# Modulation products of blocks 2 to 4 on the vector engine, an output product accumulated over two row blocks, and expert 0 with 64 slots: a diffusion layer with experts on one core

## The chip, the core and the metric

The kernel runs on one core of a Trainium2 chip. The metric is the device time of one execution in microseconds (us), the median of several runs. Everything is float32 in memory. The names of the engines are those of the profile: PE is the tensor engine (PEld its weight loads), DVE the vector engine, ACT the scalar engine, POOL the GpSimd, SP the queue that issues the weight loads.

## What is computed

One layer over 256 tokens of 2048 channels. A conditioning vector gives six modulation vectors of 2048 (mod[0] to mod[5]); a gated short convolution and a mixture of 16 experts (top group, then top two of its four experts) follow, each with a residual and a layer norm.

```python
mod = split(silu(c) @ mod_w + mod_b, 6)          # mod_w: 2048 x 12288
h = x * (1 + mod[1]) + mod[0]
gate_b, gate_c, val = split(h @ conv_in_w, 3)    # 2048 x 6144
o = (gate_b * depthwise_conv3(gate_c * val, conv_w)) @ conv_out_w
x = layer_norm(ALPHA * x + mod[2] * o, g0, b0)
h = x * (1 + mod[4]) + mod[3]                    # routed by h @ rt_grp_w, h @ rt_exp_w
y = sum over experts e of weight[e] * ((silu(h @ gate[e]) * (h @ up[e])) @ down[e])
x = layer_norm(ALPHA * x + mod[5] * y, g1, b1)   # gate, up: 2048 x 768, down: 768 x 2048
```

Evaluated on its inputs, the reference sends 14 tokens to expert 0 and 117, 80, 78, 51 and 42 to the five most loaded of the others.

## The kernel before

All weights pass once through one stream of loads on SP, in the order in which the work uses them. A ring of 6 tiles of 1.5 MB holds them (`RING`, line 30); two more places are lent to the stream late. `get` (line 118) issues the next load when the tile that had its place has been used. So a transfer starts when an engine lets go of an older tile.

**The convolution part.** float32 is split into a rounded half (cast by ACT, line 379) and the remainder (a subtraction on DVE, line 380), and three fast products replace a slow one (`mm3`, lines 387 to 389). The first product runs over eight groups of 256 channels (times three for gate_b, gate_c, val). For groups 0 to 3 it goes in five stages over the contraction (`KGS`, line 35: 2, 2, 4, 4 and 4 blocks of 128 rows), since mod[0] and mod[1] are made block by block on the way (`acc_step`, line 442; sums in four large tiles, copied there in the first stage, added later). At the end of each stage `h_hook` (line 557) empties DVE's queue (`flush`, line 544) and makes the next blocks of the modulated input (`make_h`, line 360: ACT gives the rounded half, DVE the product again and the remainder). Groups 4 to 7 run whole, in four steps each (`full_steps`, line 453). The output product `cout_step` (line 506) takes one of four row blocks (`qt`) and one of four column blocks (`j`) at a time; each of these 16 results is multiplied by mod[2] on DVE (line 531) and added to the tokens: on DVE for row blocks 0 and 3, on POOL for 1 and 2 (lines 533 to 537).

**The modulation vectors.** mod[0] and mod[1] are products on PE with 32 identical columns (`gemv_cols`, line 226, matmul at line 258). mod[2] is made by `gemv_rows` (line 275, matmul at 285) in four pieces of 512 columns. Of the eight pieces of mod[3] and mod[4], `ON_V` (line 40) puts five on DVE: the first block of 128 rows is a multiplication on ACT, the other 15 are `scalar_tensor_tensor` of 512 columns (line 263) that wait in `queue`; `split` (line 376) runs two of them (`VN`) after each weight split. A piece takes three loads (6, 6 and 4 blocks of 128 rows). mod[5] follows later, on PE.

**The order** is written out (lines 587 to 609). `EXTRA` says how many loads of mod[2] to mod[4] are put between the steps of each of the five stages, `merge` spreads them evenly, and `BEFORE` (line 36) says how many steps are left behind `router_prep`. Here 13 loads lie in the stages, 12 of them in the last, and 23 among the steps of groups 4 to 7 and eight output steps.

**The experts.** Rank 0 is expert 0, the others are ranked by load; `CAPS` (line 43) gives the slots of each rank: four with 128, four with 64, eight with 32. `SEQ` is the order: 0, 15, 14, 1, 13, 12, 2, 11, 10, 3, 9, 4, 7, 5, 6, 8. Tokens are gathered by a product with a one-hot matrix (`gather`, line 793). An expert has 8 loads for gate and up and 4 for down, 1.5 MB each. With 128 slots (`run_expert`, line 875) half of the gate and up blocks are split into two parts and done in three fast products, the other half as float32, and the down product is split by 256 columns (lines 949 to 954) with four pairs of buffers (line 685). With 64 or 32 slots all is float32, and two or four products stand side by side in the columns of PE (lines 904 and 947). `Alone` (line 970) takes the output of an expert with 128 slots back to the tokens, `Packed` (line 995) that of two or four smaller ones together. A loop (line 1175) runs once for each block of slots that a rank lacks.

Of the kernel before, what the change touches and what calls it, by code (L numbers as in the profile page):

```python
# [9 lines left out]
F32 = mybir.dt.float32  # L10
# [4 lines left out]
ALU = mybir.AluOpType  # L15
# [18 lines left out]
EXTRA = [0, 1, 0, 0, 12]  # L34
# [16 lines left out]
# Pieces of the columns of the down product; those of the last experts end with smaller ones.  # L51
# [14 lines left out]
def trunk_kernel(  # L66
# [36 lines left out]
    # ---------------------------------------------------------------- weight stream  # L103
# [14 lines left out]
    def get(i):  # L118
        """the tile of load i, whose predecessors have been used; issues what now has a place"""
# [24 lines left out]
    def expert_loads(e, pieces=QUARTERS):  # L144
        """loads of an expert's gate and up weights, and of its down weights by pieces of the columns"""
# [19 lines left out]
    # ---------------------------------------------------------------- constants, small inputs  # L165
# [10 lines left out]
    # picks rows 0, 32, 64 and 96  # L176
# [38 lines left out]
    # arithmetic that waits for its turn on the tensor engine, and on the vector engine  # L215
# [10 lines left out]
    def gemv_cols(m, c0, n, on_vector=False):  # L226
# [3 lines left out]
        nb, k0 = n // P, c0 // P  # L230

        def late():
            pt = aux_tile(f"gc{m}_{c0}")
            for i in range(nb):
                TE.transpose(pt[:, i * P : (i + 1) * P], box["r"][:, i * P : (i + 1) * P], ident)
            sm = const.tile([P, 4], F32, tag="gsum", bufs=2, name=f"gs{m}_{c0}")
            V.tensor_reduce(out=sm[:, :nb], in_=pt[:, :n].rearrange("p (i c) -> p i c", i=nb)[:, :, :: 1 if on_vector else 32],
                            axis=AX.X, op=ALU.add)
            V.scalar_tensor_tensor(
                out=modT[:, m, k0 : k0 + nb], in0=sm[:, :nb], scalar=1.0 if m in (1, 4) else 0.0,  # L240
                in1=modbT[:, m * KT + k0 : m * KT + k0 + nb], op0=ALU.add, op1=ALU.add)

        per = min(KT, 3072 // n)
        for t0 in range(0, KT, per):
            nt = min(per, KT - t0)

            def work(w, t0=t0, nt=nt):
                if t0 == 0:
                    if on_vector:
                        box["r"] = p1.tile([P, 512], F32, tag="rows", bufs=2, name=f"rows{m}{c0}")  # L250
                    else:
                        box["ps"] = aux_tile(f"gv{m}_{c0}")
                for k in range(nt):
                    kt = t0 + k
                    g = kt % 4
                    ws = w[:, k * n : (k + 1) * n]
                    if not on_vector:
                        TE.matmul(box["ps"][32 * g : 32 * g + 32, :n], sT[:, kt : kt + 1].to_broadcast([P, 32]), ws, start=kt < 4, stop=kt >= 12)  # L258
                    elif kt == 0:
                        S.mul(box["r"][:, :n], ws, sT[:, kt : kt + 1])  # L260
                    else:
                        def fn(ws=ws, kt=kt):
                            V.scalar_tensor_tensor(out=box["r"][:, :n], in0=ws, scalar=sT[:, kt : kt + 1],  # L263
                                                   in1=box["r"][:, :n], op0=ALU.mult, op1=ALU.add)
                            if kt == KT - 1:
                                pending.append(late)
                        queue.append(fn)
                if t0 + nt == KT and not on_vector:
                    box["r"] = p1.tile([P, 512], F32, tag="rows", bufs=2, name=f"rows{m}{c0}")
                    S.copy(box["r"][:, :n], box["ps"][:, :n])  # L270
                    pending.append(late)
# [963 lines left out]
```

## Time and profile before

| what | us |
|---|---|
| median of 3 runs (1347.04 to 1348.72) | 1348.4 |
| span of the profiled execution, first to last instruction | 1343.3 |
| PE busy | 1190.9 |
| DVE busy | 724.2 |
| ACT busy | 404.6 |

The runs are timed from outside the span; the profiled execution itself has no other time than its span, 5.1 us less than the median. Matmuls are pipelined, so a busy PE may also be waiting a little; how fast it goes is read from the starts of its matmuls. A window of the profile gives the busy time of every engine, the clock granted to PE (1.00 is 2.4 GHz), the share of the DMA engines and the rate in GB/s, for a stretch of time.

### The profile page before, as it was taken

How to read it: one execution, taken by the hardware profiler on the slowest of the kernel's cores; microseconds unless marked ns; L12 is line 12 of the kernel's file. 1: busy time of each engine (PE TensorE's matmuls, PEld its weight loads, DVE VectorE, ACT ScalarE, POOL GpSimd, SP SyncE). 2: the span in 40 equal slices, each digit the busy share in tenths (PEclk: the TensorE clock that was granted, in tenths of full speed). 3: DMA queues.
4: the chain of work that ended last, by engine and by line, in shares of the span. 5: the costliest groups of instructions: out<-in, count | busy, mean ns of one | idle time of the engine just before them, and what ended most of it. 6: DMA issues, size and time to landing. Idle time of an engine off the chain costs nothing. (4 is left out here: it accounts for less than half of the span.)

```text
span 1343.3 us, 23490 instructions
## 1 busy us (share of the span) xinstructions
PE 1190.9 (89%) x9429; PEld 856.0 (64%) x9429; DVE 724.2 (54%) x1526; ACT 404.6 (30%) x795; POOL 30.3 (2%) x60
## 2 busy tenths in 40 slices
PE   4999999999999999998789878997689888898883
PEld 2778876978699875775367446774267454554553
DVE  2665565597789878686266434583147321122217
ACT  1333333434244334563035223451026110100020
POOL 0000000000400120000000000000000000000000
PEclk7999999999999999999889899998789899999996
DMA  9999879799989879979999899989999999999992
GB/s 321 354 396 395 298 279 398 276 310 351 357 312 337 296 280 342 364 263 365 413 414 347 316 414 411 400 304 381 412 412 393 336 412 412 413 371 414 412 410 78
DMA packets 240947, 475.85 MB, mean 354 GB/s; under 512 B 10968, under 2 KB 74680, under 8 KB 240576
## 3 DMA queue, kind: packets, MB, share of 16 engines
q1 hardware_dynamic: 235808, 471.88, 93.2%
q10 hardware_dynamic: 5024, 2.40, 0.6%
q8 instruction: 76, 1.25, 0.3%
q14 instruction: 39, 0.32, 0.1%
HBM read 472.16 MB, written 2.10 MB: 353 GB/s over the span
## 5 line engine op out<-in xcount | busy, mean ns | idle before, releaser
L904 PE MATMUL gue<-w,xgp 128*32 128x384 f32 (+1 forms) x1536 | 218.1, 554 | 71.2 <-DMA w<-in_ex_w_up_dram 59.0
L387 PE MATMUL ci<-hhi,hic 128*128 128x256 f32 x768 | 221.1, 289 | 2.7 <-ACT hic L379 1.4
L389 PE MATMUL ci<-hhi,loc 128*128 128x256 f32 x768 | 218.6, 286 | 3.6 <-DVE loc L380 3.5
L388 PE MATMUL ci<-hlo,hic 128*128 128x256 f32 x768 | 217.9, 284 | 0.8 <-DVE hlo L374 0.7
L904 PEld LDWEIGHTS gue<-w,xgp 128*32 128x32 f32 (+1 forms) x1536 | 83.1, 130 | 197.8 <-issue 83.0
L693 DVE TENSOR_TENSOR parts<-w,parts 128x256 fp32r<-128x256 f32 (+1 forms) x320 | 135.3, 475 | 73.2 <-ACT parts L692 70.4
L692 ACT CAST parts<-w 128x256 fp32r<-128x256 f32 (+1 forms) x320 | 131.3, 449 | 114.5 <-PE gue L901 72.7
L379 ACT CAST hic<-w 128x1024 fp32r<-128x1024 f32 (+1 forms) x108 | 102.5, 954 | 183.2 <-PE ci L388 159.0
L387 PEld LDWEIGHTS ci<-hhi,hic 128*128 128x128 f32 x768 | 145.1, 189 | 14.9 <-issue 8.4
L389 PEld LDWEIGHTS ci<-hhi,loc 128*128 128x128 f32 x768 | 145.2, 190 | 9.5 <-DVE loc L380 6.0
L388 PEld LDWEIGHTS ci<-hlo,hic 128*128 128x128 f32 x768 | 146.4, 191 | 5.6 <-DVE hlo L374 2.5
L380 DVE TENSOR_TENSOR loc<-w,hic 128x1024 fp32r<-128x1024 f32 (+1 forms) x108 | 118.7, 1108 | 35.2 <-ACT hic L379 35.0
L921 ACT COPY gse<-gue 128x384 f32<-128x384 f32 x16 | 7.7, 480 | 314.8 <-PE gue L904 314.8
L904 PE MATMUL gue<-w,xfp 128*128 128x384 f32 x256 | 93.9, 498 | 2.5 <-DMA w<-in_ex_w_gate_dram 2.5
L1014 DVE TENSOR_TENSOR Y<-dne,m 32x128 f32<-32x128 f32 (+2 forms) x176 | 52.6, 299 | 42.3 <-PE dne L947 39.3
L448 DVE TENSOR_TENSOR acc<-acc,ci 128x512 f32<-128x512 f32 x48 | 33.0, 687 | 60.4 <-PE ci L389 60.4
L822 PE MATMUL gap<-ohp,xt 128*128 128x128 f32 x512 | 63.6, 279 | 1.7 <-DVE xtp L837 1.0
L822 PEld LDWEIGHTS gap<-ohp,xt 128*128 128x128 f32 x512 | 59.5, 192 | 8.7 <-issue 4.2
L258 PE MATMUL gv<-w,sT 128*32 128x512 f32 (+1 forms) x416 | 57.6, 569 | 8.2 <-DMA w<-in_mod_w_dram 8.2
L904 PEld LDWEIGHTS gue<-w,xfp 128*128 128x128 f32 x256 | 48.3, 194 | 23.5 <-issue 3.9
L263 DVE SCALAR_TENSOR_TENSOR rows<-w,sT,rows 128x512 f32<-128x512 f32 x75 | 57.9, 773 | 1.3
L954 PE MATMUL dne<-parts,ahe 128*128 128x256 f32 x192 | 57.6, 300 | 0.3 <-DVE parts L693 0.2
(302 smaller groups left out, 1679.8 us busy)
## 6 DMA issues: line engine op xcount, KB each, us to landing
w<-in_ex_w_gate_dram SPq DMA_DIRECT2D x64, 1536.0 KB, 13.6
w<-in_ex_w_up_dram SPq DMA_DIRECT2D x64, 1536.0 KB, 15.6
w<-in_ex_w_down_dram SPq DMA_DIRECT2D x60, 1536.0 KB, 15.0
w<-in_mod_w_dram SPq DMA_DIRECT2D x48, 1536.0 KB, 9.3
w<-in_conv_in_w_dram SPq DMA_DIRECT2D x84, 512.0 KB, 6.9
w<-in_mod_w_dram SPq DMA_DIRECT2D x22, 1024.0 KB, 8.0
w<-in_conv_out_w_dram SPq DMA_DIRECT2D x16, 1024.0 KB, 6.9
w<-in_conv_in_w_dram SPq DMA_DIRECT2D x24, 256.0 KB, 7.2
```

The lines of the kernel that those rows point to most:

```text
L258: TE.matmul(box["ps"][32 * g : 32 * g + 32, :n], sT[:, kt : kt + 1].to_broadcast([P, 32]), ws, start=kt < 4, stop=kt >= 12)
L263: V.scalar_tensor_tensor(out=box["r"][:, :n], in0=ws, scalar=sT[:, kt : kt + 1], in1=box["r"][:, :n], op0=ALU.mult, op1=ALU.add)
L379: S.copy(hi[:, :n], src)
L380: V.tensor_sub(lo[:, :n], src, hi[:, :n].bitcast(F32))
L387: TE.matmul(ps, whi, ahi, start=start, stop=False)
L388: TE.matmul(ps, whi, alo, start=False, stop=False)
L389: TE.matmul(ps, wlo, ahi, start=False, stop=stop)
L692: S.copy(hi[:, :n], src)
L693: V.tensor_sub(lo[:, :n], src, hi[:, :n].bitcast(F32))
L822: TE.matmul(ps[:, k * n : (k + 1) * n], xn[:, h, (k0 + k) * P : (k0 + k + 1) * P], oh[:, h, :n], start=h == 0, stop=h == 1)
L904: TE.matmul(dst, big[0][:, KF.index(kt), :] if cc == 128 else xg[:, kt, :cc], src, start=st_, stop=sp_)
L954: TE.matmul(o, a[i], lo[:, :256], start=False, stop=sp_ and m == 1)
```

## The change

1. mod[2], mod[3] and mod[4] are all made on DVE, in pieces of 1024 columns (`WIDE`): six pieces of 15 `scalar_tensor_tensor` each, six loads for a piece (five with 3 blocks of rows, one with 1). Sums over the partitions are products with a column of ones (`col_sums`, `mod2_rows`). `drain` runs two queued products after a split while more than three wait, otherwise one. `EXTRA` puts 12 loads (all of mod[2]) in the stages.
2. An output step keeps its result in PSUM over two row blocks, so there are 8 results to multiply and add; all first ones stand within group 4, behind a `flush`, the others behind group 7. `router_prep` has four steps of group 7 and eight output steps behind it.
3. ACT takes over the second product in `make_h` and the first stage's copies.
4. Expert 0 has 64 slots, as a pack of its own with an empty half.
5. The down product with 128 slots is split by 512 columns, with three pairs of buffers.

Removed comments and unchanged lines are left out of the diff:

```diff
-EXTRA = [0, 1, 0, 0, 12]
+EXTRA = [0, 1, 0, 3, 8]
-VN = 2
-ON_V = [[0, 1, 0, 1], [0, 1, 1, 1]]
+WIDE = 1024
-CAPS = [128, 128, 128, 128, 64, 64, 64, 64] + [32] * 8
+CAPS = [64, 128, 128, 128, 64, 64, 64, 64] + [32] * 8
...
-    out = []
+    out = [[SEQ[0]] + [None] * (P // CAPS[SEQ[0]] - 1)]
     for cap in (32, 64):
-        rs = [r for r in SEQ if CAPS[r] == cap]
+        rs = [r for r in SEQ[1:] if CAPS[r] == cap]
...
+    def col_sums(m, c0, n, rows_, ones_):
+        pt, nb, k0 = aux_tile(f"gc{m}_{c0}"), n // P, c0 // P
+        for i in range(nb):
+            TE.matmul(pt[:, i : i + 1], rows_[:, i * P : (i + 1) * P], ones_, start=True, stop=True)
+        V.scalar_tensor_tensor(
+            out=modT[:, m, k0 : k0 + nb], in0=pt[:, :nb], scalar=1.0 if m in (1, 4) else 0.0,
+            in1=modbT[:, m * KT + k0 : m * KT + k0 + nb], op0=ALU.add, op1=ALU.add)
...
+    def gemv_vector(m, c0, done):
+        box = {}
+        per = 3072 // WIDE
+        for t0 in range(0, KT, per):
+            nt = min(per, KT - t0)
+            def work(w, t0=t0, nt=nt):
+                for k in range(nt):
+                    kt = t0 + k
+                    ws = w[:, k * WIDE : (k + 1) * WIDE]
+                    if kt == 0:
+                        box["r"] = mod2b[:, c0 : c0 + WIDE] if m == 2 else big_tile(f"rows{m}{c0}")[:, :WIDE]
+                        S.mul(box["r"], ws, sT[:, kt : kt + 1])
+                        continue
+                    def fn(ws=ws, kt=kt):
+                        V.scalar_tensor_tensor(out=box["r"], in0=ws, scalar=sT[:, kt : kt + 1], in1=box["r"],
+                                               op0=ALU.mult, op1=ALU.add)
+                        if kt == KT - 1:
+                            pending.append(lambda: done(box["r"]))
+                    queue.append(fn)
+            yield mod_load(m, c0, WIDE, t0, nt), work
...
+    def mod2_rows(c0, r):
+        for i in range(WIDE // 512):
+            q = c0 // 512 + i
+            rq, o = r[:, i * 512 : (i + 1) * 512], slice(32 * q, 32 * q + 32)
+            V.tensor_tensor(out=rq[o], in0=rq[o], in1=bias_rows[2][o], op=ALU.add)
+            ps = aux_tile(f"gb2{q}")
+            TE.matmul(ps[:, :], onesF.to_broadcast([P, P]), rq, start=True, stop=True)
+            S.copy(mod2b[:, q * 512 : (q + 1) * 512], ps[:, :])
...
-                V.tensor_scalar(out=ht, in0=src, scalar1=sc, scalar2=sh, op0=ALU.mult, op1=ALU.add)
+                S.activation(ht, src, AF.Identity, bias=sh, scale=sc)
...
-        for fn in queue[:VN]:
-            fn()
-        del queue[:VN]
+        drain(2 if len(queue) > 3 else 1)
...
-                    V.tensor_copy(accs[g][:, a, :], pss[a][:, :])
+                    S.copy(accs[g][:, a, :], pss[a][:, :])
...
+    def cout_steps(half):
+        out = []
+        for j in range(4):
+            pso = []
+            for qt in (2 * half, 2 * half + 1):
...
+                                first, last = (qt % 2, pr, k) == (0, 0, 0), (qt % 2, pr, k) == (1, 1, 1)
...
+                    if qt % 2 == 0:
+                        return
+                    if half and j > 0:
+                        router_part(j - 1)
                     for h in range(2):
...
+                        V.tensor_mul(tmp, pso[h][:, :], mod2b[:, j * 512 : (j + 1) * 512])
+                        if half == 0:
+                            V.scalar_tensor_tensor(out=xs, in0=xs, scalar=ALPHA, in1=tmp, op0=ALU.mult, op1=ALU.add)
+                        else:
+                            V.tensor_add(xs, xs, tmp)
+                            V.bn_stats(stats[:, h, j, :], xs)
...
-    late = [st for m in (2, 3, 4) for q in range(4) for st in mods(m, q)]
+    late = [st for m in (2, 3, 4) for q in range(D // WIDE) for st in mods(m, q)]
...
-        qt = [cout_step(g - 4, j) for j in range(4)] if 4 <= g < 7 else []
-        if g < 6:
-            rest += fs[:2] + qt + fs[2:]
-        elif g == 6:
-            rest += fs
-        else:
-            rest += fs + qt_last
-        qt_last = qt
+        if g == ACC_GROUPS:
+            fs = fs[:2] + [(None, lambda w: flush())] + cout_steps(0) + fs[2:]
+        rest += fs
     steps += merge(rest[:-BEFORE], late) + [(None, lambda w: router_prep())]
-    steps += merge(rest[-BEFORE:] + [cout_step(3, j) for j in range(4)], last[:EARLY])
+    steps += merge(rest[-BEFORE:] + cout_steps(1), last[:EARLY])
...
-            hi, lo = parts[turn_of["n"] % 4]
+            hi, lo = parts[turn_of["n"] % 3]
...
-                    for m in range(2):
-                        hi, lo = split(ws[:, 256 * m : 256 * m + 256], 256)
-                        o = ps[:, 256 * m : 256 * m + 256]
-                        TE.matmul(o, a[i], hi[:, :256], start=st_ and m == 0, stop=False)
-                        TE.matmul(o, al[i], hi[:, :256], start=False, stop=False)
-                        TE.matmul(o, a[i], lo[:, :256], start=False, stop=sp_ and m == 1)
+                    hi, lo = split(ws, n)
+                    TE.matmul(ps[:, :n], a[i], hi[:, :n], start=st_, stop=False)
+                    TE.matmul(ps[:, :n], al[i], hi[:, :n], start=False, stop=False)
+                    TE.matmul(ps[:, :n], a[i], lo[:, :n], start=False, stop=sp_)
...
+                    if None in rs:
+                        G.memset(self.state[rs[0]], 0.0)
...
+                    y = self.y[p0 : p0 + cc, c : c + f]
+                    if self.first:
+                        S.copy(y, ps[p0 : p0 + cc, :f])
...
+                    if self.first:
+                        V.tensor_copy(o, ps[:, :n])
```

## Rows read from the trace of the kernel before

**Rows 1.** The page: busy time, share of the span, and the rate in 40 slices

```profile
PE 1190.9 (89%) x9429; PEld 856.0 (64%) x9429; DVE 724.2 (54%) x1526; ACT 404.6 (30%) x795; POOL 30.3 (2%) x60
GB/s 321 354 396 395 298 279 398 276 310 351 357 312 337 296 280 342 364 263 365 413 414 347 316 414 411 400 304 381 412 412 393 336 412 412 413 371 414 412 410 78
```

**Rows 2.** Windows: busy us of each engine, PE's granted clock, DMA share, GB/s

```profile
20.00:130.00 110.00, 104.81 (x810) 79.78 (x810) 59.66 (x101) 34.92 (x52) 0.00 (x0) 0.95 1.05 373
130.00:181.00 51.00, 50.75 (x400) 42.21 (x399) 29.96 (x43) 17.93 (x22) 0.00 (x0) 1.00 0.88 317
181.00:245.00 64.00, 59.58 (x446) 42.88 (x446) 39.68 (x55) 22.22 (x32) 0.00 (x0) 1.00 0.95 348
245.00:448.00 203.00, 199.85 (x1439) 177.19 (x1439) 164.46 (x205) 78.37 (x87) 13.52 (x8) 1.00 0.90 316
448.00:511.00 63.00, 61.06 (x304) 43.12 (x302) 49.66 (x70) 20.46 (x24) 13.40 (x8) 1.00 0.81 288
...
637.00:722.00 85.00, 69.86 (x599) 47.78 (x598) 39.54 (x109) 19.37 (x44) 0.00 (x0) 0.92 1.03 410
722.00:765.00 43.00, 40.32 (x293) 28.25 (x291) 28.36 (x72) 20.68 (x60) 0.00 (x0) 1.00 0.84 296
...
872.00:914.00 42.00, 40.28 (x292) 28.22 (x290) 28.06 (x71) 20.33 (x59) 0.00 (x0) 1.00 0.86 305
```

**Rows 3.** Windows as in rows 2: expert 0 to 15, two experts with 64 slots

```profile
525.00:636.00 111.00, 104.55 (x775) 76.57 (x773) 82.27 (x217) 56.91 (x146) 0.00 (x0) 1.00 0.89 338
1080.00:1170.00 90.00, 75.25 (x594) 41.21 (x594) 15.11 (x50) 8.29 (x22) 0.00 (x0) 0.96 1.04 413
```

**Rows 4.** Timeline of PE and SP, expert 0: start us, us, engine line operation

```profile
529.11 0.81 PE L904 MATMUL gue<-w,xfp 128*128 128x384 f32 x2
...
540.63 20.30 SPq L159 DMA_DIRECT2D w<-in_ex_w_down_dram  x4
...
601.51 1.50 PE L904 MATMUL gue<-w,xgp 128*32 128x384 f32 x16
```

**Rows 5.** Groups of instructions by form: count | busy us, mean ns | idle before

```profile
L904 PE MATMUL gue<-w,xgp 128*64 128x384 f32 x512 | 96.9, 513 | 22.4 <-DMA w<-in_ex_w_up_dram 20.5 <-DMA w<-in_ex_w_gate_dram 2.0
...
L947 PE MATMUL dne<-w,ae__9984 128*64 128x256 f32 x96 | 11.5, 384 | 0.2 <-DVE ae__9984 L935 0.2
...
L263 DVE SCALAR_TENSOR_TENSOR rows<-w,sT,rows 128x512 f32<-128x512 f32 x75 | 57.9, 773 | 1.3
```

**Rows 6.** Timeline of PE: a load of mod[0] and the matmul behind it

```profile
100.32 1.92 PE L258 MATMUL gv<-w,sT 128*32 128x512 f32 x14
102.16 0.39 PE L387 MATMUL ci<-hhi,hic 128*128 128x256 f32 x1
```

**Rows 7.** Timeline of ACT: casts one split apart, output steps and input steps

```profile
267.45 1.05 ACT L379 CAST hio<-w 128x1024 fp32r<-128x1024 f32 x1 [3.85 <-PE co L525]
270.17 1.05 ACT L379 CAST hio<-w 128x1024 fp32r<-128x1024 f32 x1 [1.67 <-PE co L525]
...
366.74 1.05 ACT L379 CAST hic<-w 128x1024 fp32r<-128x1024 f32 x1 [1.83 <-PE ci L388]
369.62 1.04 ACT L379 CAST hic<-w 128x1024 fp32r<-128x1024 f32 x1 [1.83 <-PE ci L388]
```

**Rows 8.** Timeline of DVE: remainders and queued products, back to back

```profile
287.21 1.23 DVE L380 TENSOR_TENSOR loc<-w,hic 128x1024 fp32r<-128x1024 f32 x1
288.34 0.75 DVE L263 SCALAR_TENSOR_TENSOR rows<-w,sT,rows 128x512 f32<-128x512 f32 x1
289.00 0.69 DVE L531 TENSOR_TENSOR t<-co,mod2b 128x512 f32<-128x512 f32 x1
...
296.32 2.33 DVE L263 SCALAR_TENSOR_TENSOR rows<-w,sT,rows 128x512 f32<-128x512 f32 x3
```

**Rows 9.** Timeline of PE: down product of expert 0, split by 256 columns

```profile
581.05 0.28 PE L952 MATMUL dne<-parts,ahe 128*128 128x256 f32 x1
581.17 0.28 PE L953 MATMUL dne<-parts,ale 128*128 128x256 f32 x1
```

More of the change, by code (lines that the diff above doesn't have):

```diff
@@ L224, in mod_load, with gemv_cols @@
         return load
-    def gemv_cols(m, c0, n, on_vector=False):
-        box = {}
[L230 to L241, printed above, removed]
+    def col_sums(m, c0, n, rows_, ones_):
[5 more added lines that the diff above has]
+            in1=modbT[:, m * KT + k0 : m * KT + k0 + nb], op0=ALU.add, op1=ALU.add)
+    def gemv_cols(m, c0, n):
+        box = {}
         per = min(KT, 3072 // n)
@@ L255, in work @@
                     g = kt % 4
[L256 to L271, printed above, removed]
-            yield mod_load(m, c0, n, t0, nt), work
+                    TE.matmul(box["ps"][32 * g : 32 * g + 32, :n], sT[:, kt : kt + 1].to_broadcast([P, 32]),
+                              w[:, k * n : (k + 1) * n], start=kt < 4, stop=kt >= 12)
@@ new lines, in work @@
+                if t0 + nt == KT:
+                    r = p1.tile([P, 512], F32, tag="rows", bufs=2, name=f"rows{m}{c0}")
+                    S.copy(r[:, :n], box["ps"][:, :n])
+                    pending.append(lambda: col_sums(m, c0, n, r, selG))
+            yield mod_load(m, c0, n, t0, nt), work
+    def gemv_vector(m, c0, done):
[18 more added lines that the diff above has]
+            yield mod_load(m, c0, WIDE, t0, nt), work
@@ new lines, in cout_steps, with load, work @@
+    def cout_steps(half):
[3 more added lines that the diff above has]
+            for qt in (2 * half, 2 * half + 1):
+                def load(w, qt=qt, j=j):
+                    nc.sync.dma_start(
+                        w[:, :2048].rearrange("p (t c) -> p t c", c=512),
+                        rows(cout[qt * 512 : (qt + 1) * 512, j * 512 : (j + 1) * 512]),
+                    )
+                def work(w, qt=qt, j=j, pso=pso):
+                    if qt % 2 == 0:
+                        pso.extend(mm_tile(f"co{half}{j}{h}") for h in range(2))
+                    for pr in range(2):
+                        hi, lo = split(w[:, pr * 1024 : (pr + 1) * 1024], 1024, f"o{qt}{j}{pr}")
+                        yh, yl = yhi[qt * 2 + pr], ylo[qt * 2 + pr]
+                        for k in range(2):
+                            for h in range(2):
+                                a, b = h * P, (h + 1) * P
+                                wh, wl = hi[:, k * 512 : (k + 1) * 512], lo[:, k * 512 : (k + 1) * 512]
+                                first, last = (qt % 2, pr, k) == (0, 0, 0), (qt % 2, pr, k) == (1, 1, 1)
+                                TE.matmul(pso[h][:, :], yh[:, k, a:b], wh, start=first, stop=False)
+                                TE.matmul(pso[h][:, :], yl[:, k, a:b], wh, start=False, stop=False)
+                                TE.matmul(pso[h][:, :], yh[:, k, a:b], wl, start=False, stop=last)
+                    if qt % 2 == 0:
+                        return
+                    if half and j > 0:
+                        router_part(j - 1)
+                    for h in range(2):
+                        xs = xt[:, h, j * 512 : (j + 1) * 512]
+                        tmp = p1.tile([P, 512], F32, tag="e", bufs=3, name=f"t{half}{j}{h}")
+                        V.tensor_mul(tmp, pso[h][:, :], mod2b[:, j * 512 : (j + 1) * 512])
[4 more added lines that the diff above has]
+                            V.bn_stats(stats[:, h, j, :], xs)
+                    if half and j == 3:
+                        router_part(3)
+                out.append((load, work))
+        return out
@@ L972, in trunk_kernel, with __init__ @@
             turn = 0
-            def __init__(self, pr, wr, name, first=False, then=None):
-                self.name, self.first, self.then = name, first, then
+            def __init__(self, pr, wr, name, then=None):
+                self.name, self.then = name, then
                 self.st = scatter_matrix(pr, wr, name)
@@ L979, in __call__ @@
                 y = y_tile()
-                if self.first:
-                    S.copy(y[:, :n], ps[:, :n])
-                else:
-                    V.tensor_tensor(out=y[:, :n], in0=ps[:, :n], in1=m5_cols(0, P, c0, n), op=ALU.mult)
+                V.tensor_tensor(out=y[:, :n], in0=ps[:, :n], in1=m5_cols(0, P, c0, n), op=ALU.mult)
                 for h in range(2):
@@ L1000, in __init__ @@
                 self.rs, self.turn, self.name, self.then = rs, rs.index(r), name, then
-                self.last = r == rs[-1]
+                self.last = r == [x for x in rs if x is not None][-1]
+                self.first = rs[0] == SEQ[0]
                 if self.turn == 0:
@@ L1141, in trunk_kernel @@
         xgs = {}
-        pack_of = {r: rs for rs in packs() for r in rs}
+        pack_of = {r: rs for rs in packs() for r in rs if r is not None}
         def places(r):
@@ L1163, in trunk_kernel @@
             if CAPS[r] == 128:
-                out_r = Alone(*places(r), f"e{r}_", r == SEQ[0], then)
+                out_r = Alone(*places(r), f"e{r}_", then)
             else:
```

80 lines of the change are left out of this document (24 added, 56 removed).

## The prediction

> **What bounds the kernel now.** I read the page first, for the busy times and the rate of the loads in slices [rows 1]: PE is busy for 89% of the span, but the rate says more. Up to about 600 us it lies between 263 and 398 GB/s, then it stands near 412 for most of the rest. So there are two parts. The windows show it [rows 2]: from 130 to 511 us PE is busy nearly all the time and the loads run at 288 to 348 GB/s, so that work sets the pace and places in the ring come free late. From 637 to 722 us the loads run at 410 GB/s while PE is busy for 70 of 85 us: there the loads set the pace, and whatever PE saves buys nothing. Inside this second part lie islands, the experts with 128 slots (722 to 765, 872 to 914), where PE is full and the rate falls to about 300. Expert 0, the first of that kind, and what follows it have 338 GB/s over 111 us with PE at 94%, against 413 where two experts with 64 slots run [rows 3].
>
> The third thing to see is DVE. Between 245 and 448 us it is busy for 164 of 203 us [rows 2]. The change puts more work there, so I count both engines step by step.
>
> **The change, part by part.** The sum is made against the span of 1343.3 us; the median is 5.1 above it, and I carry these 5.1 over unchanged, so differences are set against 1348.4.
>
> *Expert 0 with 64 slots.* Before, it holds PE from 529.1 us until expert 15 starts at 601.5 [rows 4], 72 us. With 64 slots it needs what a ranked expert of that size needs: a quarter of 96.9 us for gate and up, 24, and 11.5 for the down product [rows 5]; with taking back and transposes some 42 us (estimate, the last 6 by what is left over). Its 12 loads need 12 x 1.57 MB / 413 = 46 us. So the loads set the pace at once, and the gain is what the ring lost: the queue on SP needed 20.3 us to issue expert 0's four down loads alone [rows 4]. From 525 to 636 us 111 x 338 = 37.5 MB came in [rows 3]; at 413 that takes 90.8 us. Gain **20.2 us**, all later work moving forward as a block, since the loads bound it. At 403 GB/s the gain would be 18, at 416 it would be 21. The clearing of its pack's empty half on POOL waits for a place that one of its own up loads holds; nothing but the first copy of the down product waits for it, so I cost it at nothing (if late, expert 0's first down piece is late by it). One more copy on ACT per piece lies beside the loads.
>
> *Down product split by 512.* A matmul of 256 columns starts 0.12 us after the last [rows 9]; 144 of them make 17.3 us per expert. Of 512 columns, the output steps show 12 matmuls between casts 2.72 us apart [rows 7], 0.227 each: 72 make 16.3. So 1.0 us for each of experts 1 to 3, and only they, in the islands: up to 3 us gained. Against it stands one buffer pair less for gate and up: if the fourth split of each of 8 blocks came 0.25 us late, 3 x 8 x 0.25 = 6 us lost. While PE does the float32 block in between, three splits are made and the fourth has three triples' time, so I take **-1.5**, half of the gain, between -3 and +4.
>
> *Modulation blocks 2 to 4, PE's side.* A load with six blocks holds PE from 100.32 to 102.16 [rows 6], 1.84 us, so a piece of 16 blocks 4.9. Seven pieces leave PE: 34.3 us. If PE alone counted, this would be the gain.
>
> *The same, DVE's side.* A remainder of 1024 columns lasts 1.23 us, but the next instruction starts 1.13 after it; a product of 512 columns has the next behind it after 0.66, and three dependent ones take 2.33, 0.78 each [rows 8]. No row has a product of 1024 columns. It is at least the remainder's 1.13 and at most two dependent halves, 1.55; I take 0.78 + (1.13 - 0.66) = 1.25, as the row nearest in kind with the other's slope. 90 of them are 112 us, for 57.9 before [rows 5].
>
> By the Trainium skill (VectorE: DVE Perf Modes, "The DRAIN you can't avoid") the next instruction does not start until the pipeline is empty. The rows show starts that overlap by 0.1 us, as far as they are independent, so the trace decides for 1.13; by the rule every remainder would cost its 1.23, and the sum below would be some 8 us longer.
>
> Now the steps. An input step has three splits 2.88 us apart, 8.64 us of PE; an output step two of 2.72, 5.44 [rows 7]. In these paces the stretch from 181 to 448 us (267 us) less four input steps that are moved behind it (34.6) is 232.4: 16 input steps 138.3, eight output steps 43.5, the products 34.3 less one early load 1.8, and 18.1 for sums, hooks and waits.
> - Fourth stage (130 to 181): three loads, nine products, are put behind its third step and must all be done before the hook's remainders: 11.3 us of DVE on top of 7 in a step where PE has some 10. Between 0 and 7.7 us late, taken **+4**.
> - Last stage: per step DVE has 3.4 for remainders, 2.0 for three sums, 3.7 for the convolution's seven small operations: 9.1. With 0, 4, 6 and 6 products behind the splits the four steps take 9.1, 14.1, 16.6 and 16.6 us, 56.4, where PE needs 34.6.
> - Two input steps: 17.3, PE. The flush before the output steps: three products, 3 us (4 less what PE still has).
> - Eight output steps: per column block four remainders 4.5, four operations on the result 2.6, 5.7 products 7.1: 14.3, for PE's 10.9. Times four, 57.2.
> - Ten input steps: DVE has 3.4 + 3.6 for 2.9 products + 0.9 = 7.9, PE 8.64: 86.4. Loads: 1.57 + 1.6 MB per 8.64 us, 367 GB/s, under what they can.
> - Of the 18.1 I keep half, 9, as it can lie beside DVE's work.
>
> Together 229.3 against 232.4: **-3.1**. Ahead of 130 us one load less on PE (-1.8), and ACT twice per block in `make_h` rather than ACT and DVE (at most 0.6 us per hook, some +0.8): **-1**. From 448 to 511 us, the four moved steps beside the same output steps: DVE is busy for 50 of 63 us now and loses the half of the multiplications, and the 16 additions on POOL, which wait rather than are waited for, go: 0. So the convolution part changes by **-0.1 us**: what PE saves, DVE takes. Its bounds: if DVE's work were spread so well that only its sum counts, -15; with 5% of friction over these 230 us, +12.
>
> Sum: 1348.4 - 20.2 - 1.5 - 0.1 = **1326.6**.
>
> **The rivals.**
> 1. *DVE hides everything*, PE's 34.3 us are gained whole: 1348.4 - 20.2 - 1.5 - 34.3 = 1292. For it: DVE is idle for 39 of 203 us. Against: in the last stage 16.6 us of DVE stand in a step of 8.64. Chance 0.09.
> 2. *DVE's queue stands in PE's way* in every step, and it is slower than before. The place is the split: PE needs the next remainder, and up to two products are ahead of it. In my sum DVE goes beyond PE by 21.8 + 13.7 + 4 = 39.5 us, 32 bare products of the 88 from the fourth stage on. Each more costs 1.25, and the 21.8 us gained are gone with 17 more, at 49. All 88 bare would be 1397; half of the rest, 28 more, 1362. For it: products are queued ahead of the next split. Against: the products stand behind the remainder of their own split [rows 8], and PE is full now at a DVE share of 81% [rows 2]. Chance 0.08.
> 3. *The loads come no sooner*, because gathering for the next four experts holds the ring as expert 0 did: 1348.4 - 1.6 = 1347. For it: the rate is still low behind 600 us, as the slices show. Against: those 17 us hold two loads at most. Chance 0.06.
> 4. *PE's clock falls in expert 0*, since PE now waits for loads. Stretches with such waits have 0.92 and 0.96 on the mean [rows 2, 3], so only part of the time is at 1.2 GHz; were all of it, 42 us would become 84, 12 over the 72 of before, 1359. The loads keep 413 GB/s in those stretches. Chance 0.02. The Trainium skill (TensorE: Matmul & The Clock Gate, "HAM oscillation") has this as a rule: a tensor engine that waits between loads falls back to half its clock and starts the next block cold.
> 5. *More than 64 tokens for expert 0* would run the loop at the end, over 72 us more with nothing ahead of it: past 1400. The reference sends 14. Chance 0.01.
>
> **How the numbers follow.** My case has 0.74, and nearly all of it lies between 1309 and 1342: the convolution's bounds carry most of that, the other two parts 10 us. To leave out no more than 2 in 10 I take 1305 to 1344, which takes in a part of rivals 1 and 2. About 0.2% (2.7 us) is what a measurement of this kernel can tell from no change. Faster by more than that: my case but for a sliver, and rival 1, with what of rival 3 still gains: 0.85. Within: 0.06, mostly rival 3. Slower: rivals 2, 4 and 5 with the sliver, 0.09.
>
> **What would show it.** Right: the rate is at 405 or more from expert 0's start until experts 1 to 3; expert 15 starts about 25 us sooner after expert 0 than before; the convolution part ends at about the same time, with DVE over 90% in the last stage and the output steps and ACT's casts there 3.5 us apart rather than 2.7; products of 1024 columns last 1.25 to 1.3 us; the down product of experts 1 to 3 shrinks by 1 us or less each. Wrong: expert 0 starts 20 us or more away from 529, or its loads stay under 370 GB/s.

## The result, and the profile after

The changed kernel takes **1379.6 us** (median of 4 runs, 1377.5 to 1380.1; the kernel before in the same comparison 1347.7). The ratio is 1.0242, 95% interval 1.0223 to 1.0261. 1326.6 was forecast, so the sign was wrong and the time lies outside the range. The profiled execution has a span of 1377.5 us.

The page, as in [rows 1]: busy time, share of the span, and the rate in 40 slices.

```profile
PE 1168.6 (85%) x8991; PEld 842.6 (61%) x8991; DVE 704.5 (51%) x1308; ACT 376.2 (27%) x661; POOL 5.1 (0%) x45
GB/s 313 368 376 367 307 293 238 304 379 349 345 308 331 121 320 258 398 396 379 396 398 350 315 397 393 390 292 381 396 394 386 332 395 394 394 379 396 395 394 100
```

PE is busy for 22 us less than before, as the change meant. DVE is busy for 20 us less in all: it has 19 us more up to expert 0 and 37 us less in expert 0. But the rate in the last two thirds, where the loads set the pace, stands near 395 GB/s where it stood near 412. I had not thought of anything that could change that figure.

The windows, in the stretches of [rows 2]: busy us of PE, PEld, DVE, ACT, POOL, then PE's granted clock, DMA share, GB/s.

```profile
130.00:181.00 51.00, 47.97 (x396) 41.13 (x396) 28.92 (x38) 22.77 (x33) 0.00 (x0) 1.00 0.92 323
181.00:245.00 64.00, 43.36 (x291) 40.07 (x291) 55.58 (x66) 18.13 (x23) 0.00 (x0) 0.83 0.73 259
245.00:448.00 203.00, 180.46 (x1202) 165.16 (x1203) 175.58 (x181) 70.84 (x77) 0.00 (x0) 0.93 0.94 336
448.00:511.00 63.00, 63.00 (x420) 54.96 (x418) 36.13 (x43) 23.36 (x25) 0.00 (x0) 0.97 0.62 216
```

PE, which was busy for 259 of the 267 us from 181 to 448, is now busy for 224 and DVE for 231: PE waits. Its granted clock, 1.00 in all of these stretches before, has fallen in three of them.

Three marks of the trace divide the loss: the first matmul of expert 0, that of expert 15, and the end of the span.

| kernel | expert 0 starts | expert 15 starts | end of span |
|---|---|---|---|
| before | 529.1 | 601.5 | 1343.3 |
| after | 561.6 (+32.5) | 615.6 (+14.1) | 1377.5 (+34.2) |

So the convolution part, forecast at -0.1, loses 32.5 us; expert 0 gains 18.4 of the 20.2; and the rest of the experts, on which nothing was to happen but -1.5, loses 20.1. Two things were to be explained.

### The profile page after: what moved, and what is told of

Read it like the earlier page. It is cut to its first block, busy times and chain, and to the rows that moved or that the text cites. A ratio compares the mean times of both kernels' runs of the same rounds, so it can differ in the third digit from the quotient of the medians.

```text
span 1377.5 us, 21992 instructions
## 1 busy us (share of the span) xinstructions
PE 1168.6 (85%) x8991; PEld 842.6 (61%) x8991; DVE 704.5 (51%) x1308; ACT 376.2 (27%) x661; POOL 5.1 (0%) x45
## 5 line engine op out<-in xcount | busy, mean ns | idle before, releaser
L932 PE MATMUL gue<-w,xgp 128*32 128x384 f32 (+1 forms) x1664 | 245.9, 561 | 79.3 <-DMA w<-in_ex_w_up_dram 68.4
L932 PEld LDWEIGHTS gue<-w,xgp 128*32 128x32 f32 (+1 forms) x1664 | 95.7, 132 | 219.9 <-issue 91.1
L410 PEld LDWEIGHTS ci<-hhi,hic 128*128 128x128 f32 x768 | 152.9, 199 | 21.8 <-ACT hic L404 17.0
L405 DVE TENSOR_TENSOR loc<-w,hic 128x1024 fp32r<-128x1024 f32 (+1 forms) x108 | 118.6, 1104 | 49.5 <-ACT hic L404 49.4
L717 DVE TENSOR_TENSOR parts<-w,parts 128x384 fp32r<-128x384 f32 (+1 forms) x168 | 98.6, 613 | 63.3 <-ACT parts L716 62.5
L716 ACT CAST parts<-w 128x384 fp32r<-128x384 f32 (+1 forms) x168 | 91.4, 559 | 100.6 <-PE gue L929 68.6
L276 DVE SCALAR_TENSOR_TENSOR rows<-w,sT,rows 128x1024 f32<-128x1024 f32 x60 | 76.8, 1282 | 0.9
L932 PE MATMUL gue<-w,xfp 128*128 128x384 f32 x192 | 71.8, 504 | 2.3 <-DMA w<-in_ex_w_gate_dram 2.3
L846 PE MATMUL gap<-ohp,xt 128*128 128x128 f32 (+1 forms) x512 | 62.6, 278 | 0.7 <-DVE xgp L814 0.7
L554 PE MATMUL co<-loo,yh 128*128 128x512 f32 x128 | 51.6, 412 | 8.7 <-DVE loo L405 8.6
L404 ACT CAST hio<-w 128x1024 fp32r<-128x1024 f32 x32 | 33.5, 1048 | 74.7 <-PE co L553 60.7
L552 PE MATMUL co<-hio,yh 128*128 128x512 f32 x128 | 52.4, 409 | 0.0
## 6 DMA issues: line engine op xcount, KB each, us to landing
w<-in_ex_w_down_dram SPq DMA_DIRECT2D x60, 1536.0 KB, 15.8
```

Source lines behind the costliest of these rows:

```text
L276: V.scalar_tensor_tensor(out=box["r"], in0=ws, scalar=sT[:, kt : kt + 1], in1=box["r"], op0=ALU.mult, op1=ALU.add)
L404: S.copy(hi[:, :n], src)
L405: V.tensor_sub(lo[:, :n], src, hi[:, :n].bitcast(F32))
L410: TE.matmul(ps, whi, ahi, start=start, stop=False)
L552: TE.matmul(pso[h][:, :], yh[:, k, a:b], wh, start=first, stop=False)
L716: S.copy(hi[:, :n], src)
```

## The experiments

**The rate of the loads.** The addresses of the tiles, read from the two built programs, differ in one thing that concerns the loads: before, the ring of load tiles starts at byte 98816 of each partition, after at 98752. The change gave up two small tiles of column sums, 32 bytes each with their padding, that lay ahead of the ring. 98816 is a multiple of 256 and 512; 98752 is 192 bytes beyond a multiple of 256. In `a_align` 64 unused bytes stand ahead of the ring of the changed kernel, in `b_shift` 448 and in `b_shift256` 256 ahead of that of the kernel before:

```diff
     stats = const.tile([P, 2, 4, 6], F32, name="stats")
+    const.tile([P, 16], F32, name="pad")
```

> The changed kernel with 64 unused bytes per partition ahead of the ring, so that its first tile starts at 98816 (193 x 512) as in the kernel before, not at 98752. Theory 'place': the ring's start, 64 bytes below a multiple of 512, makes every load some 4% longer (gate loads land 3.91 us apart after, 3.76 before); then here gate loads land 3.76 apart, the load-bound stretches have 410 to 413 GB/s, expert 15 to the end takes 742 us or less instead of 762, and the time is 1345 to 1360. Theory 'work': the loads are slower by what the engines do or by the chip; then 395 GB/s and 1379 as it was.

> The kernel before with 448 unused bytes ahead of the ring, which so starts at 99264, 64 bytes below a multiple of 512, as in the changed kernel. Theory 'place': the load-bound stretches fall from 412 to 395 GB/s, expert 15 to the end takes some 25 us more, and the time is 1365 to 1385. Theory 'work': 1348, no change.

> The kernel before with 256 unused bytes ahead of the ring (99072, a multiple of 256 but not of 512). If the loads want a multiple of 512, 1360 to 1366 as with 99264 and some 395 GB/s; if a multiple of 256 is enough, 1345 to 1349 and 412 GB/s.

Measured: `a_align` 1358.4 us (ratio to before 1.0078, 1.0053 to 1.0102), 21.2 less than the changed kernel; `b_shift` 1363.5 (1.0122, 1.0106 to 1.0139), 16 more than before and just under the range expected, as its stretch from expert 15 to the end grew by 22 us, not 25; `b_shift256` 1343.7 in its one run, no slower than before. The windows of one load-bound stretch, first before:

```profile
1085.00:1165.00 80.00, 65.25 (x391) 32.33 (x389) 9.27 (x32) 3.77 (x9) 0.00 (x0) 0.96 1.04 413
```

The kernel before with the ring at 99264 (192 beyond a multiple of 256), and at 99072 (a multiple of 256, not of 512):

```profile
1085.00:1165.00 80.00, 63.66 (x553) 35.42 (x552) 14.67 (x49) 7.39 (x19) 0.00 (x0) 0.96 1.04 396
```

```profile
1085.00:1165.00 80.00, 65.26 (x392) 32.48 (x391) 9.13 (x32) 3.75 (x9) 0.00 (x0) 0.96 1.04 413
```

The changed kernel, and the same with the ring at 98816:

```profile
1085.00:1165.00 80.00, 60.63 (x590) 35.22 (x592) 16.70 (x56) 9.15 (x24) 0.00 (x0) 0.96 1.04 393
```

```profile
1085.00:1165.00 80.00, 65.33 (x590) 37.43 (x583) 16.20 (x54) 8.18 (x21) 0.00 (x0) 0.96 1.04 412
```

The last figure is the one to read: 413 or 412 wherever the ring starts at a multiple of 256, 393 to 396 where it starts 192 bytes beyond one, with the engines no busier. Theory 'place' holds, and a multiple of 256 is enough. The median distance between the landings of two neighbouring loads (from 640 us on, where they follow each other without a wait, less than 4.5 us apart) says the same: gate and up loads, rows of 3072 bytes, 3.77 us apart before, 3.92 after, 3.77 in `a_align`; down loads, rows of 2048 bytes, 3.84, 4.06 and 3.84. The shorter rows lose more, 5.8% against 4.1%, as they would if each row paid a fixed amount: 0.15 us over the 512 rows of the one load and 0.22 over the 768 of the other are both 0.29 ns a row.

The Trainium skill has a rule that fits (DMA: Bandwidth & Descriptors, "How a descriptor splits into AXI transactions"): a descriptor is cut into pieces of 256 bytes, and one that does not start at a multiple of 256 fetches the bytes ahead of its start too, for nothing. The page says so of bytes that are fetched; here the side that is shifted is the one written, and that the rule is the cause there is not shown. By it 192 bytes per row would cost 6.3% and 9.4% (an estimate from the page's figures); the trace agrees in kind and gives about two thirds of it.

**Which part of the change.** `b_exp` is the kernel before with the edits to the experts alone, `a_conv_al` the changed convolution part with the experts of before; both have the ring at 98816. The first lines of the edit of `b_exp` (the rest is that of points 4 and 5 of the change):

```diff
-CAPS = [128, 128, 128, 128, 64, 64, 64, 64] + [32] * 8
+CAPS = [64, 128, 128, 128, 64, 64, 64, 64] + [32] * 8
```

> The kernel before with only the changes to the experts: expert 0 with 64 slots, down products split by 512 (ring at 98816). My forecast for these two parts: -21.7, so 1326 (expert 0 to expert 15 in some 50 us instead of 72, the loads behind expert 0 at 410). Rival, the loads come no sooner: 1347. Rival, three pairs of buffers hold PE up in experts 1 to 3: 1330 to 1332.

> The changed convolution part (modulation blocks 2 to 4 on DVE, output product over two row blocks) with the experts of the kernel before, ring at 98816. If the convolution part is late by its own order on DVE, expert 0 starts 20 to 30 us later than before (529) and the time is 1368 to 1380. If it was late only because the loads were slow, expert 0 starts within 8 us of 529 and the time is 1345 to 1356.

Measured: `b_exp` **1335.4** (0.9916, 0.9896 to 0.9936), 12.0 less than before; `a_conv_al` 1377.0 (1.0215, 1.0193 to 1.0236), 29.5 more. So the experts gain 12.0 of the 21.7 that were forecast, a figure between the forecast and the rival of no gain. In `a_conv_al` expert 0 starts at 557.5: the convolution part is late by itself, with the ring in its old place. `b_exp` to `a_align` to the changed kernel is a ladder: -12.0, then +23.0 for the convolution part, then +21.2 for the address. The parts do not simply add: with expert 0 at 128 slots the convolution part costs 29.5, with 64 slots 23.0.

The windows of `b_exp`: expert 0's gate and up products, its down product, and what follows it.

```profile
531.00:563.00 32.00, 25.86 (x140) 13.16 (x138) 10.49 (x34) 5.59 (x12) 1.81 (x1) 0.95 1.04 412
563.00:587.00 24.00, 23.53 (x160) 16.99 (x160) 6.92 (x14) 3.81 (x11) 0.00 (x0) 0.93 1.01 408
587.00:630.00 43.00, 34.75 (x423) 21.06 (x421) 30.47 (x77) 13.16 (x37) 0.00 (x0) 1.00 0.90 345
```

The rate is full in expert 0, as forecast, against 338 over the whole stretch in [rows 3]. But behind it, while expert 15 runs, it is 345 again. I had set 413 for all 111 us. There the queue on SP waits for PE to let go of expert 15's loads (L909 are its products), 26 of the 43 us:

```profile
SPq L153 <- PE gue L909: 13.6, 2, 10.8
SPq L160 <- PE gue L909: 12.5, 2, 6.6
```

PE does these products in pieces: the second half of the gathering for four experts (3.8 us from 591.8) and the sums of mod[5] (from 600 to 608) stand between them. So gathering is a part of what holds the ring, not all of it. Expert 15 starts 16.4 us sooner after expert 0 than before, not 25 (14.5 sooner in all, as expert 0 starts 2 us later in this trace), and at the end of the span 13.2 are left.

**What holds PE in the convolution part.** The fourth stage of the changed kernel, DVE: products (L276) and remainders (L405).

```profile
176.97 2.60 DVE L276 SCALAR_TENSOR_TENSOR mod2b<-w,sT,mod2b 128x1024 f32<-128x1024 f32 x2
179.49 0.68 DVE L471 TENSOR_TENSOR acc<-acc,ci 128x512 f32<-128x512 f32 x1
180.08 9.21 DVE L276 SCALAR_TENSOR_TENSOR mod2b<-w,sT,mod2b 128x1024 f32<-128x1024 f32 x7
189.21 2.35 DVE L405 TENSOR_TENSOR loc<-w,hic 128x1024 fp32r<-128x1024 f32 x2
```

PE in the same stretch, a matmul that needs the first of these remainders:

```profile
190.48 0.58 PE L412 MATMUL ci<-hhi,loc 128*128 128x256 f32 x1 [9.93 <-DVE loc L405]
```

In the code `split` writes the remainder first and then runs two products. So by the code two products stand ahead of this remainder, the second of its step; the other seven follow behind it, five of them in the hook's flush. On DVE all nine stand ahead of it: the order on an engine is set when the program is built, and is not that of the code. By what rule the builder sets it is not shown here. PE waits 9.93 us, and that is not all. A window of the wait and two behind it:

```profile
181.00:190.40 9.40, 0.00 (x0) 0.00 (x0) 9.19 (x9) 0.00 (x0) 0.00 (x0) 0.56 1.02 370
190.40:195.00 4.60, 4.52 (x21) 4.53 (x22) 1.16 (x2) 0.00 (x0) 0.00 (x0) 0.50 1.06 392
195.00:200.00 5.00, 5.00 (x42) 5.00 (x41) 3.32 (x4) 2.10 (x2) 0.00 (x0) 0.92 0.31 82
```

While PE stands idle its granted clock falls to half (1.2 GHz), and it stays there until about 195.8: 21 matmuls in 4.6 us, and then 42 in 5. Some 25 matmuls start 0.213 us apart instead of 0.117, 2.4 us on top of the wait. The Trainium skill (TensorE: Matmul & The Clock Gate, "HAM oscillation") has the rule, that a tensor engine which waits starts its next block cold; the trace agrees, with those numbers. In [rows 2] the clock was 1.00 here.

In `a_ord` an edge of order, without a wait, keeps each product behind the remainder of its split. In `a_extra` three loads of mod[2] move from the fourth stage into the last. Both have the ring at 98816.

```diff
-        V.tensor_sub(lo[:, :n], src, hi[:, :n].bitcast(F32))
-        drain(2 if len(queue) > 3 else 1)
+        sub = V.tensor_sub(lo[:, :n], src, hi[:, :n].bitcast(F32))
+        with tc.issue_after(sub.ins):
+            drain(2 if len(queue) > 3 else 1)
```

```diff
-EXTRA = [0, 1, 0, 3, 8]
+EXTRA = [0, 1, 0, 0, 11]
```

> The changed kernel with the ring at 98816, and every product queued on DVE placed behind the remainder of the split that drains it (an edge of order alone, no wait). Theory 'order': in the program as built, up to nine products stand ahead of a remainder that PE waits for (9.8 us of PE waiting in stage four, 5.4 us in group 5), so the convolution part gets 10 to 17 us shorter, expert 0 starts at 544 to 551 instead of 561, and the time is 1341 to 1349 instead of 1358. Theory 'sum': DVE's work in these stages is the bound in any order; then at most 5 us are gained, 1353 to 1358.

> The changed kernel with the ring at 98816, and the three loads of mod[2] moved from stage four to the last (EXTRA 0, 1, 0, 0, 11). Stage four takes 47 to 49 us as before instead of 60. Theory 'sum': the last stage is bound by DVE and takes 11 us more with the nine products (55 to 66), net -1 to -3, 1355 to 1357. Theory 'order': the last stage has room, it grows by 0 to 4, net -8 to -12, 1346 to 1350.

Measured: `a_ord` 1346.9 (1.0002, 0.9979 to 1.0025), 11.5 less than `a_align`; expert 0 starts at 549.4. Both lie where theory 'order' put them. DVE in the fourth stage of `a_ord`, where the fence above has nine products in a row:

```profile
178.05 1.22 DVE L405 TENSOR_TENSOR loc<-w,hic 128x1024 fp32r<-128x1024 f32 x1
179.19 1.28 DVE L276 SCALAR_TENSOR_TENSOR mod2b<-w,sT,mod2b 128x1024 f32<-128x1024 f32 x1
180.38 1.22 DVE L405 TENSOR_TENSOR loc<-w,hic 128x1024 fp32r<-128x1024 f32 x1
181.52 2.60 DVE L276 SCALAR_TENSOR_TENSOR mod2b<-w,sT,mod2b 128x1024 f32<-128x1024 f32 x2
```

The stage takes 48.7 us instead of 60.1, as much as the whole gain. Three of the nine products run in it and the other six later; the last stage grows by 3.6 us. Of the 31.8 us by which expert 0 starts late in `a_align`, order is 11.5, a third.

`a_extra` is at 1362.9 (1.0114, 1.0082 to 1.0146), 4.5 *more* than `a_align`: its fourth stage takes 47 us instead of 60, but the last one 71 instead of 55, worse than either theory expected. The last stage has 13 products more there, not nine (27 for 14), and most of PE's waiting in it (22.5 us) is for casts of ACT, which stand behind operations of the convolution on ACT that wait 15.8 us for DVE.

The windows of `a_ord`: last stage, two steps of group 4 with the flush, eight output steps.

```profile
185.00:243.00 58.00, 43.79 (x293) 40.09 (x293) 54.88 (x67) 18.76 (x24) 0.00 (x0) 0.91 0.81 287
243.00:269.00 26.00, 21.71 (x153) 19.68 (x152) 25.87 (x29) 10.12 (x13) 0.00 (x0) 0.93 0.78 295
269.00:324.00 55.00, 49.53 (x220) 39.84 (x219) 52.56 (x52) 17.73 (x17) 0.00 (x0) 0.94 0.94 355
```

DVE is busy for 133 of these 139 us, PE for 115: DVE has next to no room left. Whether DVE alone sets the time here is another question, which the next runs bear on.

**What the products and their loads cost.** `a_noprod` leaves out the products of mod[2] to mod[4] on DVE, all but the first block; `a_noload` leaves out, besides, 47 of the 50 MB that are loaded for them (50.3 MB less the first of 16 blocks of rows; the text below, written before the run, has 45). Neither computes the modulation vectors. The first edit is that of both, the second that of `a_noload`:

```diff
                     def fn(ws=ws, kt=kt):
-                        V.scalar_tensor_tensor(out=box["r"], in0=ws, scalar=sT[:, kt : kt + 1], in1=box["r"],
-                                               op0=ALU.mult, op1=ALU.add)
...
-            yield mod_load(m, c0, WIDE, t0, nt), work
+            yield mod_load(m, c0, 16 if t0 else WIDE, t0, 1), work
```

> The changed kernel with the ring at 98816 that leaves out the products of mod[2] to mod[4] on DVE (but the first block, on ACT); all loads, sums and waits for them stay. It shows what the products cost in all. If they alone make the convolution part late, expert 0 starts about 34 us before 529, at 490 to 500, and the time is 1285 to 1297. If the other edits of that part (ACT in place of DVE, two row blocks in PSUM, the order of the loads) cost too, expert 0 starts at 505 or later.

> As a_noprod (no products of mod[2] to mod[4] on DVE), and the loads of these blocks are cut too: the first block of rows of each piece stays, every other load brings 64 bytes per partition, so 45 of 50 MB are left out. a_noprod had PE rid of 34 us of work, and expert 0 still started at 526.6 instead of the 490 to 500 that PE alone would give. Theory 'loads': the product loads, bunched in stage four, the last stage and the eight output steps, then set the pace; without them expert 0 starts at 490 to 505 and the eight output steps take 43 to 48 us instead of 59. Rival 'order or PSUM': the steps wait for something else (two row blocks in PSUM, DVE's other work); then expert 0 starts at 515 to 527.

Measured, one run each: `a_noprod` 1329.4, expert 0 at 526.6; `a_noload` 1291.7, expert 0 at 490.7. The eight output steps, first without the products, then without the loads too:

```profile
259.00:318.00 59.00, 53.30 (x240) 43.36 (x239) 26.86 (x30) 17.81 (x17) 0.00 (x0) 0.91 0.92 343
```

```profile
236.00:282.00 46.00, 46.00 (x225) 38.70 (x224) 27.03 (x29) 18.08 (x18) 0.00 (x0) 1.00 0.64 215
```

With the loads, eight steps take 59 us and PE waits though DVE has only 27 us to do; without, 46 and PE is full. So the 34 us that leave PE are real (529.1 to 490.7 is 38), and the loads take back 36 of them before DVE does one product, 34 of these in the fourth and the last stage and the eight output steps. The rest, 526.6 to 560.9, comes with the products. But 59 is what the loads give in this order and not a limit of theirs: `a_ord`, with all loads and all products, does the eight output steps in 55. So loads and products both hold these steps, and a part of each cannot be told from the other.

**A better order.** `a_ord_rp` is `a_ord` with `router_prep` behind group 7, where it was before; `a_ord_rp_x` is that with `EXTRA` 0, 1, 2, 3, 6; `b_exp_ord` is `b_exp` with the edge of order.

```diff
-    steps += merge(rest[:-BEFORE], late) + [(None, lambda w: router_prep())]
-    steps += merge(rest[-BEFORE:] + cout_steps(1), last[:EARLY])
+    steps += merge(rest, late) + [(None, lambda w: router_prep())]
+    steps += merge(cout_steps(1), last[:EARLY])
```

> As a_ord, with router_prep behind the last step of group 7 (where it was before) instead of ahead of that group's first, and the late loads spread over four more steps. Theory 'flush': router_prep empties DVE's queue (five products, sums, four router operations) ahead of a remainder, which makes the step behind it 20 us long instead of 8.6; moved, these 11 us are gone, 1333 to 1338. Rival 'moved on': the output step behind it waits as long, 1344 to 1348.

> As a_ord_rp, with two loads of mod[2] from the last stage into stage three (EXTRA 0, 1, 2, 3, 6). DVE is busy for 55 of 58 us in the last stage and for about half of stage three. If DVE's sum is the bound of the last stage, six products fewer there give 5 to 8 us: 1326 to 1332. If stage three's loads are the bound (344 GB/s and PE busy for 47 of 49 us), it gets longer by as much: 1333 to 1340.

> As b_exp (convolution part of before, expert 0 with 64 slots, down split by 512), with the products on DVE behind the remainder of their split. In the kernel before PE waits 3.5 us for remainders over the whole run, so at most that is to be gained: 1331 to 1335. If the order edges cost DVE idle time, 1337 to 1345.

Measured: `a_ord_rp` 1342.2 (0.9964, 0.9951 to 0.9978), between the two theories: the first step of group 7 shrinks from 20.0 to 9.2 us, but from the first output step behind it to expert 0 it takes 88.1 us instead of 81.3, and expert 0 starts only 4.9 us sooner (544.5). `a_ord_rp_x` 1352.2 (1.0048, 1.0029 to 1.0066), over both ranges: the third stage grew by 6.7 us, as its rival said, and the last one took 64 us instead of 59. But this run is no test of DVE's sum in the last stage, since the products did not leave it. Counted by where they start on DVE:

| run | products in the last stage | its length, us |
|---|---|---|
| `a_noprod` | 0 | 51.6 |
| `a_align` | 14 | 54.8 |
| `a_ord_rp_x` | 18 | 64.2 |
| `a_ord` | 19 | 58.4 |
| `a_ord_rp` | 19 | 59.2 |
| `a_extra` | 27 | 70.7 |

Two loads fewer took one product out of the stage, 19 to 18; the two steps with the flush have five fewer, the third stage four more and the fourth two more. Why the stage took 5 us more with one product fewer stays open. The others grow with their products, but from 51.6 us without any. `b_exp_ord` 1340.7 (0.9968, 0.9945 to 0.9991), 5 *more* than `b_exp`, in the range of its second case: with the short products of before the builder's order was the better one; that DVE stands idle for it is not shown. So the fastest version is `b_exp`, 1335.4: the experts' edits alone.

## Why the prediction was wrong, point by point

The miss of 53.0 us is 21.2 for the address of the ring, 23.1 for the convolution part (+23.0 where -0.1 was forecast) and 9.7 for the experts (-12.0 where -21.7 was forecast), less 1.0 by which the kernel before was faster in the later comparisons. The prediction's own sign of being wrong came true: expert 0 starts 32.5 us away from 529. The steps of the convolution part are compared in `a_align`, whose ring stands where it stood before; a step starts with its first cast on ACT.

- **The address of the ring** has no term in the sum, and is 21 of the 53 us of the miss. Nothing in the rows of before could show it; the diff could, since it takes away tiles that lie ahead of the ring, and where a tile lies can be worked out without running anything. I read the change only as operations.
- **"The same, DVE's side", the price of a product.** 1.25 was taken; the rows after say 1.28 for one, and 1.32 from start to start where each needs the one ahead of it (the seven that take 9.21 us above), so nine take 11.8 us and not 11.3:

```profile
L276 DVE SCALAR_TENSOR_TENSOR rows<-w,sT,rows 128x1024 f32<-128x1024 f32 x60 | 76.8, 1282 | 0.9
```

- **The stages where DVE was to be the bound** came out near the forecast: last stage 56.4 forecast, 54.8 measured; eight output steps 57.2 and 61.5; the two steps ahead of them with the flush 20.3 and 23.4. That is in part luck: without a product on DVE (`a_noprod`) the last stage takes 51.6 and the output steps 58.8, by the loads, which the sum did not have in these stages.
- **The rule on the pipeline** that the prediction quotes (the Trainium skill, VectorE: DVE Perf Modes, "The DRAIN you can't avoid") has its exception in the same paragraph: a next instruction that is not held starts earlier. So it does not speak against the 1.13 of the rows.
- **"Fourth stage +4"**: +12.8. Nine products stood ahead of the remainder, where I had let some of them run while PE worked off its ten us; with the wait came the slow clock. The step that failed is that overlap.
- **"Ten input steps 86.4", with 9 for friction**: 101.1, for 95.4. This is rival 2's place: one of these steps waits 5.4 us for a remainder that stands behind five products. I held against that rival that the products stand behind the remainder of their own split [rows 8], which two rows of one place could not carry.
- **"From 448 to 511: 0"**: +6.5, from group 7's start to expert 0. I had counted the operations that move, and not `router_prep`, which moves ahead of group 7 with its flush. The step behind it takes 17.7 us in the changed kernel, and on DVE stand ahead of it:

```profile
435.63 3.92 DVE L276 SCALAR_TENSOR_TENSOR rows<-w,sT,rows 128x1024 f32<-128x1024 f32 x3
...
440.06 1.27 DVE L276 SCALAR_TENSOR_TENSOR rows<-w,sT,rows 128x1024 f32<-128x1024 f32 x1
...
444.90 0.17 DVE L232 SCALAR_TENSOR_TENSOR modT<-gc,T1t 128x8 f32<-128x8 f32 x1 [1.99 <-PE gc L231]
```

  The first remainder of that step stands at 445.75, behind four products and the sums that they feed.
- **"Ahead of 130 us: -1"**: +3.6; the second stage takes 36.0 us for 31.6, and 30.8 in `a_noload`: its one load for mod[2] does it, for `a_noprod` has 36.0 too. The kernel before had a load of that size in this stage; why it did no harm there stays open.
- **"Modulation blocks 2 to 4, PE's side"**, 34.3 us: right as a figure (38 in `a_noload`), wrong as something to be had. I checked the loads' rate in the ten input steps alone; in the stages ahead of them the loads, in this order, come too late, and `a_noprod` gives 1329 where rival 1 has 1292. With this order of loads that rival could not come true, whatever DVE did; `a_noload` is at 1292.
- **Expert 0, -20.2**: -16.4 from expert 0 to expert 15 in `b_exp`, and -12.0 in the median with the point below. The mechanism was right, for the rate in expert 0 is full; the rate behind it was set too high, 413 for 345. Rival 3 had named the kind of reason (work behind expert 0 holds the ring); gathering is only a part of that work.
- **Down product by 512, -1.5**: expert 1's down product takes 21.8 us instead of 22.6, but the distance from expert 1 to expert 13 is 71.2 in `b_exp` for 71.1, so 0: the 0.9 us are lost again in expert 1. Whether to the loads or to the pair of buffers that is missing is not shown.
- POOL's clearing of the pack cost nothing, as forecast: in the changed kernel it ran from 574.2 to 576.0, 20 us ahead of the first copy.

Rival 2's 1362, given 0.08, is near what both parts give with the ring in its old place (`a_align` 1358.4), and in its place, DVE's queue. That the figures meet so well is in part luck, as 9.7 us of the way to it come from the experts. What failed in the convolution part is that the forecast had only the sum of DVE's work and no order in it, and no wait for loads in the stages ahead of the ten input steps.

## What to carry to other kernels

When an edit adds or drops a small buffer, look where the large load buffers now start: at a multiple of 256 bytes these loads ran at 413 GB/s, 192 bytes beyond one at 395, in either kernel. Before work is moved off an engine, ask in every stage what the next bound is: here the loads, in the order that they had, took back 36 of the 38 us that PE would have gained, so 2.5 were left even with the work done for nothing. And read the order of an engine's instructions in the built program, not in the code: nine products ahead of one remainder made a stage 12.8 us longer where 4 were forecast, and PE, which waited, lost its clock too.

## What was not expected of the hardware

- A start 192 bytes beyond a multiple of 256 costs loads of 1.5 MB 4.1% (rows of 3072 bytes) and 5.8% (rows of 2048 bytes); 256 bytes beyond a multiple of 512 cost nothing in the one run that had it.
- A wait of PE of 10 us had the next 25 matmuls start 0.213 us apart instead of 0.117.
